# Taking an expert's quarters two at a time, and letting six experts add their rows in memory

## The chip, the cores and the metric

The kernel runs on one core of one Trainium2 chip. Its time is the device time of that core in microseconds (us), the median of several executions. TensorE is called PE here, VectorE DVE, ScalarE ACT, GpSimd POOL and SyncE SP, as in the profile.

## What is computed

The reference is one layer of an encoder for 1024 tokens of width 1024: a LayerNorm, an input projection that feeds three mixers (retention, S5, windowed attention), an output projection with a residual and a LayerNorm, and then the part that the change touches: 16 experts that each choose 128 tokens, with a hidden width of 2048, and a last LayerNorm over all tokens.

```python
aff = jax.nn.softmax(logits, axis=-1)
gates, idx = lax.top_k(jnp.swapaxes(aff, 1, 2), cap)
xs = x[bidx, idx]
hdn = jax.nn.silu(jnp.einsum('becd,edf->becf', xs, w_gate)) * jnp.einsum('becd,edf->becf', xs, w_up)
out = jnp.einsum('becf,efd->becd', hdn, w_down) * gates[..., None]
ffn = jnp.zeros_like(x).at[bidx, idx].add(out.astype(x.dtype))
h = layer_norm(DEEPNORM_ALPHA * h + ffn, ln2_g[l], ln2_b[l])
```

All in float32. A token may be chosen by several experts, or by none; their outputs add up.

## The kernel before

The first part (up to about 460 us) computes the LayerNorm, the projections, the mixers and the routing; the change leaves it alone. From there on 16 experts run one after the other, and nearly all the time is theirs.

**Pieces.** An expert's hidden width is cut into four *quarters* of 512 columns. A quarter is six *pieces* of weights of 1 MB each (128 partitions x 2048 float32): two of the gate matrix, two of the up matrix, two of the down matrix, 384 pieces in all. PE multiplies a piece with `mm3_piece` (line 2292): each product is made from a high and a low part of both operands, as high x high, low x high and high x low, so that a piece is 12 products of 128x512. So each weight piece has to be split first. SP loads it into one of five buffers `wraw` (`Experts.load`, line 2335), ACT copies it to a rounded type, the high half (`Experts.high`, line 2352), DVE subtracts that from the raw piece, the low half (`Experts.low`, line 2361). Six buffers `whl` hold split pieces, so the splitting runs up to six pieces ahead of PE; a new piece is loaded into a raw buffer as soon as the low half that read it is made. Six pieces at the start (`WHOLE`) go to PE unsplit, by `mm_whole` (line 2300).

**A quarter.** For quarter q, PE runs steps 0 to 3 (gate, gate, up, up of q) and then steps 4 and 5 (the two down pieces of quarter q-1), in `Experts.quarter`. Around the steps stand other pieces of work, put into lists by `plan(q)` as "before" or "after" step (q, s): the silu of the gate product on ACT after step 2 (line 2396), its product with the up product on DVE after step 3 (line 2402), and, ahead of the next quarter's first step, four transposes on PE that turn the 128x512 hidden values `hid` (`turned`, line 2275), split into high and low `hT` by ACT and DVE right after that step (lines 55 and 56). Splits of tokens use the same two lines. The down products of an expert's four quarters add up in two PSUM banks `y`.

**An expert's tokens.** In experts 0 to 7 the next expert's tokens are found by `expert_hot` (DVE, line 2238) and `expert_slots` (eight small products on PE, line 2247), and their rows `xs` are gathered from memory by an indirect DMA on POOL (`expert_rows`, line 2254). In the third quarter the rows are transposed in two halves, ahead of steps 1 and 2. Alongside, experts 1 to 7 find the tokens of the expert eight further on as well; experts 8 to 14 only gather the next expert's rows.

**An expert's output.** It must be added to the rows `acc_d` in memory, which start as the scaled residual. Experts 0 to 7 do this in the store (`expert_add`): ACT scales the two halves of `y` by the gates into `eo` (line 2486), and an indirect DMA on POOL adds them in memory (line 2487). From expert 8 on, the last LayerNorm begins as well, since rows that are not chosen again are final: one of eight tiles of 128 tokens is normed beside each expert (`final_norm`: loaded as `zz<-acc_d` by SP at line 2549, stored at line 2552), and each later expert rewrites the output rows of its own tokens. So experts 8 to 14 gather their rows (`final_rows`, line 2505), DVE adds the two halves of `y` to them (`last_sum`, line 2567), POOL stores the sum to `acc_d` plainly (line 2587), and the same rows are normed (`last_norm`: ACT for mean and variance, DVE for gain and shift) and scattered to the output by POOL (line 2572). Expert 15 ends the kernel with the same in parts.

**What sets the order.** Each engine runs its instructions in the order in which the program writes them. SP's queue holds, beside the weight loads, the loads and stores of `final_norm`; an instruction that waits there holds back everything behind it. POOL's queue holds all indirect DMAs and two small operations per norm. PSUM gives the experts two banks to `y`, three to gate and up (`gu`), and three to transposes and slot products (`tp`).

Of the kernel before, what the change touches and what calls it, by code (L numbers as in the profile page):

```python
# [20 lines left out]
P = 128  # L21
# [2281 lines left out]
class Experts:  # L2303
# [7 lines left out]
    WHOLE = 0, 4, 10  # L2311
    sort = None

    def __init__(self, K, I, O):
        self.K, self.I, self.O = K, I, O
        self.order = []
        for q in range(4 * E + 1):
            e, f = divmod(q, 4)
            if q < 4 * E:
                self.order += [I[n][e, f, half] for n in ("exp_w_gate", "exp_w_up") for half in range(2)]  # L2320
            if q:
                e, f = divmod(q - 1, 4)
                self.order += [I["exp_w_down"][e, f, half] for half in range(2)]
# [60 lines left out]

    def plan(self, q):

        K, nc, pool = self.K, self.K.nc, self.K.ex
        e, f = divmod(q, 4)
        at, box = self.at, {}

        def put(name, fn):
            return lambda: box.__setitem__(name, fn())
# [5 lines left out]
        def hidden():  # L2398
            self.hT[q] = [pool.tile([P, 4, P], F32R, name=f"hT{s}", bufs=2) for s in range(2)]
            split(K, *self.hT[q], box["tp"])  # L2400
        at(self.after, q, 2, silu)
        at(self.after, q, 3, lambda: nc.vector.tensor_tensor(self.h[q], self.h[q], self.pg[q][1], OP.mult))  # L2402
        turn = (q + 1, 0 if q else 1) if q < 4 * E - 1 else (q, 5)
        at(self.before, *turn, put("tp", lambda: turned(K, self.h[q], 0)))
        at(self.after, *turn, hidden)
        if f == 0 and e + 1 < E:
            late = ((q, 0), (q, 3), (q, 3), (q + 2, 1)) if e else ((q + 2, 3), (q + 2, 5), (q + 2, 5), (q + 3, 4))
            if e < E - LAST:
                at(self.after, *late[0], put("hot", lambda: expert_hot(K, e + 1)))
                at(self.before, *late[1], put("pt", lambda: expert_slots(K, e + 1, box["hot"])))  # L2410
                at(self.after, *late[2], put("xs", lambda: expert_gather(K, e + 1, box["pt"], True)))
            else:
                at(self.after, *late[2], put("xs", lambda: expert_rows(K, e + 1)))
            for half in range(2):
                q1, s1 = late[3][0], late[3][1] + half
                at(self.before, q1, s1, put(half, lambda half=half: turned(K, box["xs"], half * 4)))
                at(self.after, q1, s1, lambda half=half: self.tokens(e + 1, half, box[half]))
        if f == 2 and 0 < e < E - LAST:
            e2 = e + LAST
            at(self.after, q, 0, put("hot", lambda: expert_hot(K, e2)))  # L2420
            at(self.before, q, 3, put("pt", lambda: expert_slots(K, e2, box["hot"])))
            at(self.after, q, 3, lambda: expert_gather(K, e2, box["pt"]))
# [9 lines left out]
        if q >= 4 * (E - LAST) and f == 0:  # L2432
            at(self.after, q + 1, 3, lambda: final_rows(K, e))

    def quarter(self, q):
        K, nc = self.K, self.K.nc
        e, f = divmod(q, 4)
        steps = []
        if q < 4 * E:
            self.plan(q)  # L2440
            self.pg[q] = [K.pg.tile([P, 512], F32, name="gu", tag="gu") for _ in range(2)]
            if f == 0:
                self.py[e] = [K.py.tile([P, 512], F32, name="y", tag="y") for n in range(2)]
            for s in range(4):
                half = s % 2
                steps.append((s, [[self.pg[q][s // 2]]] * 4,
                              lambda half=half: [[self.xT[e][r][:, half * 4 + c, :] for c in range(4)] for r in range(2)],
                              half == 0, half == 1))
        if q:
            e1, f1 = divmod(q - 1, 4)  # L2450
            for half in range(2):
                steps.append((4 + half, [self.py[e1], self.py[e1]],
                              lambda half=half: [[self.hT[q - 1][r][:, half * 2 + c, :] for c in range(2)] for r in range(2)],
                              f1 == 0 and half == 0, f1 == 3 and half == 1))
        for s, outs, a, first, last in steps:
            for fn in self.before.pop((q, s), []):
                fn()
            if self.taken in self.whole:
                mm_whole(nc, outs, [self.xF[:, s % 2 * 4 + c, :] for c in range(4)], self.whl.pop(self.taken), first, last)
            else:  # L2460
                mm3_piece(nc, outs, a(), self.whl.pop(self.taken), first, last, self.taken == len(self.order) - 1)
            for fn in self.after.pop((q, s), []):
                fn()
            if self.sort and next(self.sort, self) is self:
# [311 lines left out]
```

## Time and profile before

| | |
|---|---|
| median of 3 executions | 1581.62 us (1580.8 to 1582.26) |
| the profiled execution's own time | 1577.74 us |
| its span, first to last instruction | 1576.0 us |
| DMA traffic | 507.33 MB, of it 461.88 MB read from HBM |
| low halves on DVE (line 2361) | 378 of 2288 ns, 858.0 us |
| high halves on ACT (line 2352) | 378 of 1919 ns, 724.6 us |
| landing of a weight piece after its issue | 7.7 to 8.5 us |

The busy times of the engines overlap; what counts is which engine ends last in each stretch. The profile gives for each engine its busy time, for each group of instructions the idle time just before them and what ended it, and for the DMA queues what they moved. One piece is 1 MB, so the weights alone are 384 of those megabytes, and they are loaded in the last 1100 us. "Clock" or PEclk is the share of full speed that PE was granted.

### The profile page before, as it was taken

How to read it: one execution, taken by the hardware profiler on the slowest of the kernel's cores; microseconds unless marked ns; L12 is line 12 of the kernel's file. 1: busy time of each engine (PE TensorE's matmuls, PEld its weight loads, DVE VectorE, ACT ScalarE, POOL GpSimd, SP SyncE). 2: the span in 40 equal slices, each digit the busy share in tenths (PEclk: the TensorE clock that was granted, in tenths of full speed). 3: DMA queues.
4: the chain of work that ended last, by engine and by line, in shares of the span. 5: the costliest groups of instructions: out<-in, count | busy, mean ns of one | idle time of the engine just before them, and what ended most of it. 6: DMA issues, size and time to landing. Idle time of an engine off the chain costs nothing.

```text
span 1576.0 us, 21110 instructions
## 1 busy us (share of the span) xinstructions
PE 1553.0 (99%) x7713; PEld 1276.4 (81%) x7713; DVE 1400.0 (89%) x1726; ACT 1124.0 (71%) x1294; POOL 189.9 (12%) x244
## 2 busy tenths in 40 slices
PE   8999999999999999999999999999999999999997
PEld 6888888788866888888888888888888888888786
DVE  7986865888878989999999998989999999999996
ACT  6744455877735777777777777777877778787873
POOL 4002111111110101010100101000201201020111
PEclk9999999999999999999999999999999999999999
DMA  6556478344268999999999999999999999999993
GB/s 235 180 171 145 113 228 252 98 135 125 86 234 348 389 383 400 397 389 383 382 380 369 378 402 371 403 409 415 406 422 410 418 412 417 414 415 392 398 418 155
DMA packets 101529, 507.33 MB, mean 322 GB/s; under 512 B 12976, under 2 KB 26032, under 8 KB 50736
## 3 DMA queue, kind: packets, MB, share of 16 engines
q1 hardware_dynamic: 85120, 475.03, 77.1%
q0 software_dynamic: 16304, 30.94, 6.9%
q8 instruction: 61, 1.00, 0.2%
q14 instruction: 44, 0.36, 0.1%
HBM read 461.88 MB, written 42.99 MB: 320 GB/s over the span
## 4 chain that ended last, share of the span: by engine, by line
PE 79%; DVE 7%; DMA 7%; issue 3%; ACT 3%; SPq 0%; POOL 0%; POOLq 0%; ACTq 0%; DVEq 0%
PE gu L2292 34%; PE y L2292 17%; PE mm L64 5%; PE mm L66 5%; PE mm L65 5%; DVE whl L2361 4%; DMA wraw<-in_exp_w_down 2%; PE tp L2275 2%; DMA wraw<-in_exp_w_up 2%; PE gu L2300 1%; ACT whl L2352 1%; PE po L1521 1%; DMA wraw<-in_exp_w_gate 1%; PE tp L1501 1%; PE at L1450 1%
## 5 line engine op out<-in xcount | busy, mean ns | idle before, releaser
L2361 DVE TENSOR_TENSOR whl<-wraw,whl 128x2048 fp32r<-128x2048 f32 x378 | 858.0, 2288 | 65.3 <-ACT whl L2352 63.0
L2352 ACT ACTIVATE whl<-wraw 128x2048 fp32r<-128x2048 f32 x378 | 724.6, 1919 | 243.4 <-PE gu L2292 86.8
L2292 PE MATMUL gu<-whl,xT 128*128 128x512 f32 x3000 | 712.3, 394 | 0.0
L2292 PEld LDWEIGHTS gu<-whl,xT 128*128 128x128 f32 x3000 | 555.4, 188 | 114.6 <-issue 1.0
L2292 PE MATMUL y<-whl,hT 128*128 128x512 f32 x1536 | 359.5, 389 | 0.0
L2292 PEld LDWEIGHTS y<-whl,hT 128*128 128x128 f32 x1536 | 288.0, 188 | 59.7
L2254 POOL DMA_INDIRECT xs<-h_d,index x15 | 29.9, 1994 | 454.0 <-PE y L2292 301.4
L64 PE MATMUL mm<-hT,whl 128*128 128x512 f32 x160 | 65.4, 409 | 0.0
L65 PE MATMUL mm<-hT,whl 128*128 128x512 f32 x160 | 62.6, 391 | 0.0
L66 PE MATMUL mm<-hT,whl 128*128 128x512 f32 x160 | 62.5, 391 | 0.0
L55 ACT ACTIVATE hT<-tp 128x512 fp32r<-128x512 f32 x76 | 43.8, 583 | 16.3 <-PE tp L2275 9.8
L64 PE MATMUL mm<-WO,yh 128*128 128x512 f32 x128 | 53.4, 417 | 0.0
L56 DVE TENSOR_TENSOR hT<-tp,hT 128x512 fp32r<-128x512 f32 x76 | 51.4, 683 | 1.9 <-ACT hT L55 1.5
L66 PE MATMUL mm<-WO,yl 128*128 128x512 f32 x128 | 50.7, 396 | 0.0
L65 PE MATMUL mm<-WO,yh 128*128 128x512 f32 x128 | 50.6, 395 | 0.0
L2402 DVE TENSOR_TENSOR hid<-hid,gu 128x512 f32<-128x512 f32 x64 | 43.6, 681 | 2.2 <-PE gu L2292 2.2
L2396 ACT ACTIVATE hid<-gu 128x512 f32<-128x512 f32 x64 | 37.2, 581 | 8.6 <-PE gu L2300 8.6
L64 PE MATMUL mm<-whl,hT 128*128 128x256 f32 (+1 forms) x120 | 42.8, 356 | 0.0
L2275 PEld LDWEIGHTS tp<-ident,hid 128*128 128x128 f32 x256 | 31.5, 140 | 11.4 <-DVE hid L2402 3.4
L66 PE MATMUL mm<-whl,hT 128*128 128x256 f32 (+1 forms) x120 | 40.3, 336 | 0.4 <-DVE hT L182 0.4
L2275 PE MATMUL tp<-ident,hid 128*128 128x128 f32 x256 | 38.5, 272 | 1.9 <-DVE hid L2402 1.8
L1461 DVE CUSTOM_DVE_ANT_0 S<-at,R,sink 128x384 f32<-128x384 f32 (+1 forms) x64 | 36.8, 578 | 3.9 <-PE at L1450 3.3
(445 smaller groups left out, 1795.5 us busy)
## 6 DMA issues: line engine op xcount, KB each, us to landing
wraw<-in_exp_w_up SPq DMA_DIRECT2D x128, 1024.0 KB, 8.5
wraw<-in_exp_w_down SPq DMA_DIRECT2D x128, 1024.0 KB, 8.1
wraw<-in_exp_w_gate SPq DMA_DIRECT2D x122, 1024.0 KB, 7.7
wraw<-in_w_in SPq DMA_DIRECT2D x8, 1024.0 KB, 5.8
whole<-in_exp_w_gate SPq DMA_DIRECT2D x6, 1024.0 KB, 8.3
q_d<-kst SPq DMA_DIRECT2D x32, 128.0 KB, 2.5
wraw<-in_w_out SPq DMA_DIRECT2D x4, 1024.0 KB, 7.1
qs<-q_d POOLq DMA_DIRECT2D x16, 256.0 KB, 3.6
```

Of the source, the lines that this page charges most:

```text
L55: nc.scalar.activation(hi, src, AF.Copy)
L56: eng.tensor_tensor(lo, src, hi.bitcast(F32), OP.subtract)
L64: nc.tensor.matmul(ps, a[0], b[0], start=start, stop=False)
L65: nc.tensor.matmul(ps, a[0], b[1], start=False, stop=False)
L66: nc.tensor.matmul(ps, a[1], b[0], start=False, stop=stop)
L1461: K.nc.vector.tensor_tensor_reduce(S[g][:, :W], K.at.pop((i, g))[:, :W], K.R[:, ro:ro + W], 2.0 ** -(h + 1), K.sink[:, h:h + 1], OP.add, O ...
L2275: K.nc.tensor.transpose(pt[:, c, :], src[:, (c0 + c) * P:(c0 + c + 1) * P], K.ident)
L2292: nc.tensor.matmul(ps, a[s][c], u[:, t, i * w:(i + 1) * w], start=first and id(ps) not in began, stop=last and left[id(ps)] == 0)
L2352: self.K.nc.scalar.activation(u[:, 0, :], self.raw[k1].rearrange("p a b -> p (a b)"), AF.Copy)
L2361: self.K.nc.vector.tensor_tensor(u[:, 1, :], raw, u[:, 0, :].bitcast(F32), OP.subtract)
L2396: nc.scalar.activation(self.h[q], self.pg[q][0], AF.Silu)
L2402: at(self.after, q, 3, lambda: nc.vector.tensor_tensor(self.h[q], self.h[q], self.pg[q][1], OP.mult))
```

## The change

**Order of the pieces.** `program()` writes the order of all pieces down. The first expert stays as it was, quarter by quarter (`SINGLE`). From its end on, two quarters are taken together: gate and up of q, gate and up of q+1, the down pieces of q-2, the down pieces of q-1, twelve steps that are still counted as (q, 0) to (q, 5) and (q+1, 0) to (q+1, 5). `place(q, s)` gives the step at which piece s of quarter q stands.

**Hidden values.** The silu comes right after the first up piece as before. The product of gate and up comes after the second up piece for the second quarter of a pair, and two steps later than that for the first. Both quarters' transposes stand ahead of the next pair's first step; the two splits follow after steps 1 and 3 of that pair. `run()` replaces `quarter()`; `ahead()` does what stood at the end of its loop, and after two steps of each pair (6 and 7 of twelve) holds DVE's low halves back by two pieces.

**Tokens.** Up to expert 8 the rows are transposed at the start and in the middle of the second pair of the expert before (`turns`); the slot products for the expert eight ahead stand in that middle too. The rows of experts 9 to 15 are gathered an expert earlier than before, and transposed at the starts of the two pairs of the expert before, beside the hidden values.

**Outputs.** Experts 8 to 13 now use `late_norm`: `expert_add` adds their two halves in the store, as experts 0 to 7 do, one step later POOL gathers the summed rows (line 2643); mean and variance follow in the next quarter's steps, gain, shift and the scatter (line 2630) in the one after that. Expert 14 keeps `last_norm`, a quarter later, with its rows gathered at line 2564. In `final_norm` the tile is loaded one step later, and shift and store come up to three steps later.

After the change the splits stand at lines 2351 (high) and 2360 (low), the weight load at 2334, `expert_add` at 2545 and 2546, the tile's load at 2608 and its store at 2611.

The diff, without most of the removed lines of `plan` and `quarter`, which stand in the listing above, and without the copies of old code:

```diff
@@ -2309,18 +2309,17 @@
     WHOLE = 0, 4, 10
+    SINGLE = 4
...
@@ -2382,14 +2381,40 @@
+    def program(self):
...
+        for q in range(self.SINGLE):
+            put(6 * q, q, 0, 4)
+            if q:
+                put(6 * q + 4, q - 1, 4, 2)
+        for q in range(self.SINGLE, 4 * E, 2):
+            put(6 * q, q, 0, 4)
+            put(6 * q + 4, q + 1, 0, 4)
+            if q > self.SINGLE:
+                put(6 * q + 8, q - 2, 4, 2)
+            put(6 * q + 10, q - 1, 4, 2)
+        for i in range(2):
+            put(24 * E + 2 * i, 4 * E - 2 + i, 4, 2)
+        return out
+
+    def place(self, q, s):
+
+        if q < self.SINGLE:
+            return q, s
+        o = 6 * (q - q % 2) + 4 * (q % 2) + s
+        return o // 6, o % 6
...
-        at(self.after, q, 2, silu)
-        at(self.after, q, 3, lambda: nc.vector.tensor_tensor(self.h[q], self.h[q], self.pg[q][1], OP.mult))
-        turn = (q + 1, 0 if q else 1) if q < 4 * E - 1 else (q, 5)
-        at(self.before, *turn, put("tp", lambda: turned(K, self.h[q], 0)))
-        at(self.after, *turn, hidden)
...
+        at(self.after, *self.place(q, 2), silu)
+        late = 2 * (q >= self.SINGLE and q % 2 == 0)
+        at(self.after, *self.place(q, 3 + late), lambda: nc.vector.tensor_tensor(self.h[q], self.h[q], self.pg[q][1], OP.mult))
+        if q < self.SINGLE:
+            t = (q + 1, 0 if q else 1)
+        elif q < 4 * E - 2:
+            t = (q - q % 2 + 2, 0)
+        else:
+            t = (4 * E - 1, 4)
+        at(self.before, *t, turn)
+        at(self.after, t[0], t[1] + (q == 4 * E - 1 if t[1] else q % 2 * 2 + 1 if q >= self.SINGLE else 0), hidden)
+
+    def others(self, q):
...
+        elif f == 0 and e < E - LAST:
+            slots(e + 1, (q, 0), (q, 3), True)
+            turns(e + 1, (q + 2, 0), (q + 3, 0))
+        elif f == 2 and E - LAST - 1 <= e < E - 2:
+            at(self.after, q, 3, put("xs", lambda: expert_rows(K, e + 2)))
+            turns(e + 2, (q + 2, 0), (q + 4, 0))
         if f == 2 and 0 < e < E - LAST:
...
+            slots(e + LAST, (q, 1), (q + 1, 0), False)
         if f == 0:
             if e < E - LAST:
-                at(self.after, q + 5, 0, lambda: expert_add(K, e, self.py[e]))
+                at(self.after, q + 6, 0, lambda: expert_add(K, e, self.py[e]))
+            elif e < E - 2:
+                late_norm(self, e)
             elif e < E - 1:
                 last_norm(self, e)
...
+    def run(self):
...
+                if step:
+                    self.ahead(2 * (q >= self.SINGLE and q % 2 == 1 and s < 2))
...
+    def ahead(self, hold=0):
...
+        lead = self.taken + self.lead(self.taken)
+        self.high(min(lead + 1, self.taken + self.RING))
+        self.low(lead - hold)
+        self.taken += 1
...
-    X.at(X.after, q, 0, load)
+    X.at(X.after, q, 1, load)
     X.at(X.after, q, 5, lambda: last_mean(K, b["z"], b["y"], b["s"]))
     X.at(X.after, q + 1, 0, lambda: last_var(K, b["z"], b["y"], b["s"]))
...
+    X.at(X.after, q + 1, 2, lambda: last_gain(K, b["z"], b["y"], b["s"]))
+    X.at(X.after, q + 1, 5, lambda: last_shift(K, b["y"], b["s"]))
+    X.at(X.after, q + 2, 0, store)
...
+def late_norm(X, e):
+
+    K, b, q = X.K, {}, 4 * e + 6
+
+    def rows():
+        b["z"], b["s"] = K.ex.tile([P, D], F32, name="eo", tag="xs", bufs=3), stats_tile(K)
+        K.nc.gpsimd.indirect_dma_start(out=b["z"], out_offset=None, in_=K.acc_dram,
+                                       in_offset=bass.IndirectOffsetOnAxis(ap=K.index[:, e:e + 1], axis=0))
...
+    X.at(X.after, q, 0, lambda: expert_add(K, e, X.py[e]))
+    X.at(X.after, q, 1, rows)
+    X.at(X.after, q + 1, 2, mean)
+    X.at(X.after, q + 1, 3, lambda: last_var(K, b["z"], b["y"], b["s"]))
+    X.at(X.after, q + 2, 0, lambda: last_gain(K, b["z"], b["y"], b["s"]))
+    X.at(X.after, q + 2, 3, lambda: last_shift(K, b["y"], b["s"]))
+    X.at(X.after, q + 2, 4, lambda: last_scatter(K, X.O, e, b["y"]))
```

PE's order in a late expert before, from the last down piece of one quarter through the transposes of hidden values (`tp<-ident,hid`) and of the next expert's rows (`tp<-ident,xs`); `gu` is gate or up, `y` down, `x4` means four such instructions in a row:

```order
L2292 MATMUL y<-whl,hT_11721 128x512 x4
L2275 MATMUL tp<-ident,hid 128x128 x4
L2292 MATMUL gu<-whl,xT_11368 128x512 x4
L2292 MATMUL gu<-whl,xT_11369 128x512 x4
L2292 MATMUL gu<-whl,xT_11368 128x512 x4
L2275 MATMUL tp<-ident,xs 128x128 x4
L2292 MATMUL gu<-whl,xT_11368 128x512 x4
L2292 MATMUL gu<-whl,xT_11369 128x512 x4
L2292 MATMUL gu<-whl,xT_11368 128x512 x4
L2275 MATMUL tp<-ident,xs 128x128 x4
```

And the same engine after the change, at the seam of two pairs in a late expert, from the last two down pieces on:

```order
L2292 MATMUL y<-whl,hT_11623 128x512 x4
L2292 MATMUL y<-whl,hT_11624 128x512 x4
L2292 MATMUL y<-whl,hT_11623 128x512 x8
L2292 MATMUL y<-whl,hT_11624 128x512 x4
L2292 MATMUL y<-whl,hT_11623 128x512 x4
L2275 MATMUL tp<-ident,xs 128x128 x4
L2275 MATMUL tp<-ident,hid 128x128 x8
L2292 MATMUL gu<-whl,xT_11155 128x512 x4
```

The transposes of two quarters' hidden values and of one half of the rows now stand together, and products are cut into by transposes once in twelve pieces.

SP's order around a tile's load before, where a name in brackets is a semaphore that the instruction waits for: DMAHW counts landings of SP's own loads, DVE the low halves that free a raw buffer, DMASW4 the landing of the plain store of the expert's sum, which POOL issues six steps earlier:

```order
L2335 DMA wraw<-in_exp_w_up 128x2048 [waits DMAHW0_49,DVE_49]
L2335 DMA wraw<-in_exp_w_up 128x2048 [waits DMAHW1_49,DVE_49]
L2335 DMA wraw<-in_exp_w_down 128x2048 [waits DMAHW2_49,DVE_49]
L2549 DMA zz<-acc_d 128x1024 [waits DMASW4_49]
L2335 DMA wraw<-in_exp_w_down 128x2048 [waits DMAHW3_49,DVE_49]
L2335 DMA wraw<-in_exp_w_gate 128x2048 [waits DMAHW4_49,DVE_49]
```

And after, where DMASW3 is the landing of the adding store that POOL issues one step earlier:

```order
L2334 DMA wraw<-in_exp_w_down 128x2048 [waits DMAHW6_49,DVE_49]
L2334 DMA wraw<-in_exp_w_down 128x2048 [waits DMAHW7_49,DVE_49]
L2334 DMA wraw<-in_exp_w_down 128x2048 [waits DMAHW0_49,DVE_49]
L2334 DMA wraw<-in_exp_w_down 128x2048 [waits DMAHW1_49,DVE_49]
L2608 DMA zz<-acc_d 128x1024 [waits DMASW3_49]
L2334 DMA wraw<-in_exp_w_gate 128x2048 [waits DMAHW2_49,DVE_49]
L2334 DMA wraw<-in_exp_w_gate 128x2048 [waits DMAHW3_49,DVE_49]
```

The tile's load now stands right behind an adding store of the same memory, ahead of the next expert's gate weights.

More of the change, by code (lines that the diff above doesn't have):

```diff
@@ L2315, in __init__ @@
         self.K, self.I, self.O = K, I, O
+        self.steps = self.program()
         self.order = []
-        for q in range(4 * E + 1):
+        for _, q, s in self.steps:
             e, f = divmod(q, 4)
[L2319 to L2323, printed above, removed]
+            self.order.append(I["exp_w_gate" if s < 2 else "exp_w_up"][e, f, s % 2] if s < 4 else
+                              I["exp_w_down"][e, f, s - 4])
         self.whole = [k + i for k in self.WHOLE for i in range(2)]
@@ L2431, in plan @@
                 final_norm(self, t, q + 4 * t + 2)
[L2432 to L2436, printed above, removed]
-        e, f = divmod(q, 4)
[L2438 to L2442, printed above, removed]
-                self.py[e] = [K.py.tile([P, 512], F32, name="y", tag="y") for n in range(2)]
[L2444 to L2464, printed above, removed]
-                self.sort = None
-                K.sorted()
-            lead = self.taken + self.lead(self.taken)
-            self.high(min(lead + 1, self.taken + self.RING))
-            self.low(lead)
-            self.taken += 1
-        self.pg.pop(q - 1, None), self.h.pop(q - 2, None), self.hT.pop(q - 2, None)
@@ new lines, in product @@
+    def product(self, q, s):
+        K, nc, half = self.K, self.K.nc, s % 2
+        e, f = divmod(q, 4)
+        if s < 4:
+            if s == 0:
+                self.pg[q] = [K.pg.tile([P, 512], F32, name="gu", tag="gu") for _ in range(2)]
+            outs, a = [[self.pg[q][s // 2]]] * 4, [[x[:, half * 4 + c, :] for c in range(4)] for x in self.xT.get(e, [])]
+            first, last = half == 0, half == 1
+        else:
+            if f == 0 and s == 4:
+                self.py[e] = [K.py.tile([P, 512], F32, name="y", tag="y") for n in range(2)]
+            outs, a = [self.py[e]] * 2, [[x[:, half * 2 + c, :] for c in range(2)] for x in self.hT[q]]
+            first, last = f == 0 and half == 0, f == 3 and half == 1
+        if self.taken in self.whole:
+            mm_whole(nc, outs, [self.xF[:, half * 4 + c, :] for c in range(4)], self.whl.pop(self.taken), first, last)
+        else:
+            mm3_piece(nc, outs, a, self.whl.pop(self.taken), first, last, self.taken == len(self.order) - 1)
@@ L2708, in build @@
     K.sorted = sorted_out
-    for q in range(4 * E + 1):
-        X.quarter(q)
+    X.run()
     last_rows(X, E - 1)
```

74 lines of the change are left out of this document (49 added, 25 removed).

## The prediction

> **What bounds the kernel now.** I read the page's engine table and slices first, then busy time by stretches one expert long, then the chain of work inside one expert, and last the rows of the engines around one expert's store.
>
> ```profile
> PE 1553.0 (99%) x7713; PEld 1276.4 (81%) x7713; DVE 1400.0 (89%) x1726; ACT 1124.0 (71%) x1294; POOL 189.9 (12%) x244
> PE   8999999999999999999999999999999999999997
> PEclk9999999999999999999999999999999999999999
> DMA  6556478344268999999999999999999999999993
> ```
>
> TensorE (PE) is busy in every slice and its granted clock never falls; from a third of the span on, the DMA engines are busy all the time too. The stretches below run from one quarter's first product to the same product of the next expert, so each holds one expert's work: one early expert, then four late ones in a row.
>
> ```profile
> core 0: us, PE busy (x) PEld busy (x) DVE busy (x) ACT busy (x) POOL busy (x), PEclk, DMA share, GB/s
> 720.56:789.48 68.92, 68.92 (x330) 56.65 (x329) 63.26 (x47) 51.95 (x37) 4.96 (x2) 1.00 0.99 378
> 1217.82:1286.07 68.25, 68.25 (x314) 56.41 (x313) 65.35 (x41) 54.77 (x43) 10.72 (x8) 1.00 1.01 416
> 1286.07:1355.07 69.00, 69.00 (x317) 57.01 (x316) 66.15 (x41) 55.55 (x43) 10.50 (x8) 1.00 1.01 416
> 1355.07:1424.07 69.00, 68.46 (x313) 56.34 (x312) 64.83 (x41) 53.65 (x43) 9.99 (x8) 1.00 1.01 410
> 1424.07:1493.08 69.01, 67.71 (x310) 55.74 (x309) 64.84 (x41) 54.99 (x43) 8.61 (x7) 1.00 1.01 403
> ```
>
> Until 1286 us PE has no idle time: the expert costs what PE's instructions cost, 68.25 us. The next three take 207.01 us together, 2.26 more than three times 68.25, with 1.84 us of it as plain idle time. PE's waits from 1400 us on are one row:
>
> ```profile
> PE tp L2275 <- DVE hid L2402: 1.8, 2, 1.3
> ```
>
> PE stood before the transposes of a quarter's hidden values, whose product of gate and up VectorE (DVE) had not yet made. DVE is at 65 of 68 us there, and the quarter gives it two pieces (5.4 us) from the up product to the transposes.
>
> So two limits lie close together: PE, and the feeding of PE (weight load, ACT's high half, DVE's low half). This chain is one late expert on PE, from the quarter in which the next expert's rows are transposed:
>
> ```profile
> 1182.76 0.44 PE tp L2275 x4
> 1183.20 2.78 PE gu L2292 x12
> 1185.98 0.44 PE tp L2275 x4
> 1186.41 2.77 PE gu L2292 x12
> 1189.19 0.44 PE tp L2275 x4
> 1189.63 5.50 PE gu L2292 x24
> 1195.13 5.44 PE y L2292 x24
> 1200.57 0.44 PE tp L2275 x4
> 1201.01 10.93 PE gu L2292 x48
> 1211.94 5.44 PE y L2292 x24
> 41.31 0.87 PE tp L204 x8
> ```
>
> A piece is 12 products and takes 2.72 us undisturbed (5.44 / 2). Behind a group of transposes the first piece takes 2.77 or 2.78: each break between transposes and products costs about 0.06. The last row, from early in the program, shows that eight transposes in a row cost 0.87, twice four, and no more.
>
> **The change, term by term. First, breaks on PE.** Products and transposes stay the same in number. Before, an expert has six breaks (four quarters, two halves of the next expert's rows); now a pair of quarters begins with all its transposes. A late pair is 12 transposes, 0.44 + 0.87, then 96 gate-up products, 10.93 + 10.88 (48 behind a break, 48 without its 0.05), and 48 down products, 2 x 5.44: 34.00 us. Two pairs are 68.0 against 68.25. Over experts 1 to 15 the change removes 30 breaks before hidden values (one a pair) and 28 before rows (in the early experts one of the halves stands beside the slot products, which break there anyway): 58 x 0.06 = 3.5 us, all on PE, which is the bound. **-3.5.**
>
> **Second, slack for the hidden values.** Now the product of gate and up is ordered two pieces after the first quarter's up product, at the second one's own, and the transposes come with the next pair: at least four pieces (10.9 us) instead of two. The splits of the transposed values have some seven pieces until the down products read them. What made PE wait 2.26 us (1.84 idle, the rest drawn out) has no place left, as long as the feeding itself isn't late. **-2.3.**
>
> **Third, the sums of experts 8 to 13.** DVE's two sums go, ACT's two scalings come:
>
> ```profile
> L2567 DVE SCALAR_TENSOR_TENSOR eo<-y,gates,eo 128x512 f32<-128x512 f32 x16 | 11.3, 744 | 5.5 <-PE y L2292 5.5
> L2486 ACT ACTIVATE eo<-y,gates 128x512 f32<-128x512 f32 x16 | 10.0, 673 | 0.0
> L2238 DVE TENSOR_TENSOR hot<-slot,slots 128x512 bf16<-128x512 f32 x30 | 19.3, 683 | 0.0
> L56 DVE TENSOR_TENSOR hT<-tp,hT 128x512 fp32r<-128x512 f32 x76 | 51.4, 683 | 1.9 <-ACT hT L55 1.5
> ```
>
> An expert's DVE load falls by 2 x 0.744 = 1.5 us, ACT's rises by 1.35 of the 13 it has free: nothing on the path by itself. But the store must now add in memory, and the tile load `zz<-acc_d` (line 2608) has moved from 6 pieces behind the store to one. It is issued by SP, on the one queue that also issues every weight load, and must wait for the store to land. The nearest rows are those around expert 7's store, which adds in memory today (the first two from the chain, the next six from the timeline, the last two the landings of the adding store and of a weight load from their lines' views):
>
> ```profile
> 1029.44 0.44 PE tp L2275 x4
> 1029.87 10.94 PE gu L2292 x48
> 1029.47 1.92 ACT L2352 ACTIVATE whl<-wraw 128x2048 fp32r<-128x2048 f32 x1 [0.80 <-PE y L2292]
> 1031.30 1.25 ACT L2486 ACTIVATE eo<-y,gates 128x512 f32<-128x512 f32 x2
> 1031.42 2.29 DVE L2361 TENSOR_TENSOR whl<-wraw,whl 128x2048 fp32r<-128x2048 f32 x1 [0.42 <-ACT whl L2352]
> 1032.82 2.35 POOL L2487 DMA_INDIRECT acc_d<-eo,index  x1 [63.39 <-ACT eo L2486]
> 1033.74 3.77 SPq L2335 DMA_DIRECT2D wraw<-in_exp_w_down  x2
> 1039.68 3.04 SPq L2335 DMA_DIRECT2D wraw<-in_exp_w_gate  x2
> 1045.20 0.33 SPq L2335 DMA_DIRECT2D wraw<-in_exp_w_up  x1
> 1045.20 0.99 POOL L2505 DMA_INDIRECT eo<-acc_d,index  x1 [10.03 <-DMA acc_d<-eo,index]
> DMA to landing us min/median/max: 11.0/11.7/12.9
> DMA to landing us min/median/max: 4.8/8.1/17.2
> ```
>
> POOL waits for the landing until 1045.2. In the new order SP would stand there as well: the last weight load ahead of it goes out at 1037.2 (33.74 + 3.77, less 0.33 for one issue), the ones of 1039.7 and 1042.4 would go at 1045.6. That is a hole of 8.0 us in the issues. The load of 1037.2 keeps the DMA engines fed for about 9 (8.1 typical, more beside the store); the load behind the hole brings its data some 2.3 after its issue (the fastest landing of 4.8 less 2.5 for 1 MB at full rate). So the engines idle for 8.0 + 2.3 - 9 = 1.3 us an expert, between 0.9 and 2.5.
>
> Can the DMA engines afford that? Two stretches at the same full share:
>
> ```profile
> 1472.00:1488.00 16.00, 16.00 (x74) 13.21 (x73) 14.23 (x9) 12.62 (x11) 1.73 (x2) 1.00 1.02 427
> 1030.00:1044.00 14.00, 14.00 (x63) 11.58 (x62) 12.40 (x8) 11.08 (x9) 2.35 (x1) 1.00 1.02 386
> ```
>
> 427 GB/s is full rate; with an adding store in it the stretch moves 386, so adding costs 14 x 41 / 427 = 1.3 us of all engines. A late expert moves 416 x 68.25 = 28.4 MB, 66.5 us at 427, now 67.8 with the adding. PE wants 68.0. The feeding loses 1.3 (hole) less 0.2, about 1.1 us an expert, and falls behind by that much at each of the eight tile loads: some 9 by the end, or less, since the more it lags the longer its queue and the shorter the idle time.
>
> What covers that lag is the row of split pieces. In the rows above PE ends a piece at 1029.44 and ACT starts a high half in its buffer at 1029.47; PE reads that buffer again as its sixth piece from there, at 1029.87 + 10.94 + 2.72 = 1043.5, and DVE has its low half at 1033.71: 9.8 us ahead. Before, the hidden values spent that cover first (the wait above came at a small lag); now nothing is due sooner. Nine of lag in 9.8 of cover: I take a wait of 0.8 us in all, with bounds of 0 (idle for 0.9: 0.7 x 8 = 5.6, covered) and 9 (idle for 2.5: 2.3 x 8 = 18.4, less 9.8).
>
> [...]
>
> **Sum.** -3.5 - 2.3 + 0.8 = -5.0 us. The profiled execution took 1577.74 (its span 1576.0 and 1.74 around it), which gives 1572.7. The runs' median is 1581.62, 3.9 above the profiled one; I take that difference as unchanged, so 1576.6 for the median. A measurement of this kernel can tell about 0.2% from no change, 3.2 us.
>
> **Rivals.** *The hole starves PE.* The place is SP before `zz<-acc_d`; the price is the lag beyond the cover. Every microsecond of loss an expert above 9.8 / 8 = 1.2 puts 8 us on the end; from (9.8 + 5.8) / 8 = 1.95 the kernel is slower than before. At 2.7 (the slowest store's 12.9, which makes the idle time 2.5, and engines that fall short of PE's pace by 0.2 instead of beating it by that) it is 21.6 - 9.8 - 5.8 = +6.0: 1587.6. For it: full DMA share today, and a queue that can't pass the waiting load. [...] Against it: the lag feeds the queue. Chance 0.18.
>
> *The gain is handed back in small waits*: in experts 1 to 7 the slot products of the expert eight ahead, in the middle of the second pair, take the bank that held the second hidden values, and so wait for their split on DVE. In line from the first piece's end stand three low halves (2.29 each), the hot rows (2 x 0.683) and two splits; the third low half starts no sooner than two pieces on, so the split ends about 11.5 us on, and the bank is wanted at 13.6. Two of slack cover it, and a lag above that doesn't; in expert 1, where weights come late, it may cost 1 to 3 us once, and 0.7 each in seven experts would take 5. Time then 1579 to 1582, no change. The same end has a partly starved PE (3 to 6 us). Chance 0.22.
>
> **Numbers.** Forecast 0.60, its own range 1574.3 (both gains, no wait, some of the unprofiled runs' longer time gone too) to 1578.4. No change 0.22, slower 0.18. The range of 8 in 10 goes from 1574.3 to 1585.5, which leaves out the worst of the starved case. Faster by over 0.2%: 0.60; within: 0.22; slower: 0.18.
>
> **What would show it.** Right: a late expert of about 68.0 on PE, an early one of 68.65; no wait of `tp` for `hid`; SP's issues with a hole of about 8 us at each `zz<-acc_d`, and ACT waiting longer for weights behind it. Wrong: PE waiting for `whl` from DVE in the last experts (the hole starves), or the slot products waiting in experts 1 to 7.

## The result and the profile after

The changed kernel takes 1600.78 us (1593.6 to 1605.77, 6 runs), the kernel before 1582.08 (1580.8 to 1584.48, 6 runs): 18.7 us slower, a ratio of 1.0127 with a 95% interval of 1.0108 to 1.0146 (the quotient of the two medians, 1.0118, lies inside). Forecast were 1576.6. The profiled execution took 1603.88, with a span of 1602.2, and stands 26.1 above the profiled one before, somewhat more than the medians do.

The page's engine table and slices of the changed kernel:

```profile
PE 1561.3 (97%) x7713; PEld 1283.6 (80%) x7713; DVE 1393.4 (87%) x1714; ACT 1131.2 (71%) x1306; POOL 203.1 (13%) x244
PE   8999999999999999999999999999999998999995
DMA  5556478343178999999999999999999999999993
```

PE still looks full, but for the same 7713 instructions its busy time is 8.3 us longer: some products are drawn out or run at a lower granted clock (0.94 in the last stretch). The stretches say where. The first holds an early expert, the next five the experts 10 to 14, each from the first product of its second quarter to the same product of the next expert (us, busy time of each engine, clock, DMA share, GB/s):

```profile
743.06:811.69 68.63, 68.63 (x329) 56.93 (x328) 63.18 (x47) 52.05 (x36) 4.95 (x2) 1.00 0.99 382
1155.27:1223.28 68.01, 68.01 (x313) 56.58 (x312) 60.24 (x35) 51.95 (x42) 13.02 (x8) 1.00 1.00 395
1223.28:1292.42 69.14, 68.20 (x314) 56.56 (x312) 62.21 (x38) 53.13 (x43) 12.04 (x8) 1.00 1.00 395
1292.42:1366.98 74.56, 70.42 (x313) 57.52 (x312) 66.43 (x40) 57.90 (x46) 13.09 (x8) 0.98 0.99 393
1366.98:1436.40 69.42, 68.20 (x314) 56.57 (x313) 62.78 (x38) 53.94 (x44) 12.53 (x8) 1.00 1.00 394
1436.40:1507.76 71.36, 69.66 (x309) 55.58 (x308) 62.53 (x38) 54.93 (x44) 13.10 (x8) 1.00 1.00 393
```

The early expert takes 68.63 and the first of the late ones 68.01: PE's own instructions became as much cheaper as forecast. But the DMA engines move 393 to 395 GB/s at a full share, where it was 403 to 416 before, and after 1223 us four experts take 284.5 us instead of four times 68. The end, the last 305 products and transposes, before (first fence) and after:

```profile
1498.39:1565.76 67.37, 67.37 (x305) 55.39 (x303) 57.94 (x38) 44.35 (x35) 9.21 (x8) 1.00 0.77 319
```

```profile
1507.76:1591.97 84.21, 73.73 (x305) 57.75 (x303) 69.53 (x45) 51.36 (x41) 13.85 (x9) 0.94 0.76 299
```

The end alone loses 16.8 us. Three queues now wait where they did not before, except for two waits of POOL's, 11.5 us together (from the waits of SP and ACT after 1000 us and of POOL):

```profile
SPq L2608 <- DMA acc_d<-eo,index: 56.9, 8, 8.4
ACT zz L2582 <- DMA zz<-acc_d: 16.2, 8, 4.2
POOL eo L2643 <- DMA acc_d<-eo,index: 47.1, 5, 10.5
```

SP stands 7.1 us (56.9 / 8) before a tile's load; then ACT stands before the tile's mean, and its high halves of weights behind it. One such place, in expert 12 (timeline rows of POOL, SP, ACT and PE):

```profile
1327.12 2.38 POOL L2546 DMA_INDIRECT acc_d<-eo,index  x1 [16.53 <-ACT eo L2545]
1328.05 3.28 SPq L2334 DMA_DIRECT2D wraw<-in_exp_w_down  x2
1339.75 0.33 SPq L2608 DMA_DIRECT2D zz<-acc_d  x1
1340.17 0.87 SPq L2334 DMA_DIRECT2D wraw<-in_exp_w_gate  x2
1340.01 1.92 ACT L2351 ACTIVATE whl<-wraw 128x2048 fp32r<-128x2048 f32 x1 [3.87 <-DMA wraw<-in_exp_w_down]
1343.32 1.06 ACT L2582 ACTIVATE zz<-zz 128x1024 f32<-128x1024 f32 x1 [1.40 <-DMA zz<-acc_d]
1346.81 2.11 PE L2292 MATMUL y<-whl,hT 128*128 128x512 f32 x8 [1.19 <-ACT whl L2351]
1353.95 0.66 PE L2275 MATMUL tp<-ident,xs 128*128 128x128 f32 x4 [2.74 <-DMA xs<-h_d,index]
```

No weight load goes out between 1331.3 and 1340.2. ACT waits 3.87 us for a weight piece and 1.40 for the tile. PE then stands before a split piece, and again before the rows `xs`, whose gather went out at 1341.30, held up on POOL behind the gather that waits 10.49 us for the same store.

At the end it is worse. SP's rows around the last tile's load, and PE's two longest stands (timeline), then the landing of a last piece (from the chain):

```profile
1546.03 3.85 SPq L2334 DMA_DIRECT2D wraw<-in_exp_w_down  x2
1557.95 0.33 SPq L2608 DMA_DIRECT2D zz<-acc_d  x1
1558.37 3.01 SPq L2334 DMA_DIRECT2D wraw<-in_exp_w_down  x4
1567.23 1.11 PE L2275 MATMUL tp<-ident,hid 128*128 128x128 f32 x4 [3.64 <-DVE hid L2431]
1577.44 2.08 PE L2292 MATMUL y<-whl,hT 128*128 128x512 f32 x4 [2.76 <-ACT hT L55]
```

```profile
1561.04 13.84 DMA wraw<-in_exp_w_down
```

The last four weight loads stand behind that tile, which waits 8 us for expert 14's store. ACT and DVE take their work in the order written: the silu of the last hidden values (1565.29) comes behind the tile's mean, before which ACT waits 4.20 us, and the splits of hidden values (L55, 1576.81) come behind three high halves that wait 1.36, 1.63 and 0.51 us for their loads. PE stands behind both, for 3.64 and 2.76 us.

### The profile page after: what moved, and what is told of

The parts are those of the page before. It is cut to its first block, busy times and chain, and to the rows that moved or that the text cites. A ratio compares the mean times of both kernels' runs of the same rounds, so it can differ in the third digit from the quotient of the medians.

```text
span 1602.2 us, 21127 instructions
## 1 busy us (share of the span) xinstructions
PE 1561.3 (97%) x7713; PEld 1283.6 (80%) x7713; DVE 1393.4 (87%) x1714; ACT 1131.2 (71%) x1306; POOL 203.1 (13%) x244
## 4 chain that ended last, share of the span: by engine, by line
PE 63%; DMA 17%; DVE 9%; issue 5%; ACT 5%; POOL 0%; SPq 0%; POOLq 0%; ACTq 0%; DVEq 0%
PE gu L2292 24%; PE y L2292 12%; DVE whl L2360 6%; DMA wraw<-in_exp_w_gate 5%; PE mm L64 5%; PE mm L66 5%; PE mm L65 5%; DMA acc_d<-eo,index 4%; DMA wraw<-in_exp_w_up 3%; DMA wraw<-in_exp_w_down 2%; PE tp L2275 2%; ACT whl L2351 2%; PE gu L2300 1%; PE po L1521 1%; PE tp L1501 1%
## 5 line engine op out<-in xcount | busy, mean ns | idle before, releaser
L2292 PE MATMUL gu<-whl,xT 128*128 128x512 f32 x3000 | 698.5, 392 | 2.9 <-ACT hid L2421 1.5
L2546 POOL DMA_INDIRECT acc_d<-eo,index x14 | 32.6, 2328 | 332.1 <-ACT eo L2545 332.1
L55 ACT ACTIVATE hT<-tp 128x512 fp32r<-128x512 f32 x76 | 43.7, 583 | 11.6 <-PE tp L204 6.7
L2630 POOL DMA_INDIRECT out<-yl,index x8 | 31.3, 3912 | 117.4 <-DVE hT L56 93.5
```

Of the source, the lines that this page charges most:

```text
L55: nc.scalar.activation(hi, src, AF.Copy)
L2292: nc.tensor.matmul(ps, a[s][c], u[:, t, i * w:(i + 1) * w], start=first and id(ps) not in began, stop=last and left[id(ps)] == 0)
L2546: nc.gpsimd.indirect_dma_start(out=K.acc_dram, out_offset=bass.IndirectOffsetOnAxis(ap=K.index[:, e:e + 1], axis=0), in_=o, in_offset=None ...
```

## The experiments

The theory after this profile: the *hole* on SP (the time in which it issues no load) starves PE. The rival: the *adding* stores take so much of the DMA engines that the weights come late wherever the tile's load stands. A third, the *pairs* themselves, came in when both were found to be true and not enough.

The ratio in each row is against the kernel before, in runs on the same chip; different rows can come from different chips, so rows are compared by their ratios. A ratio can differ from the quotient of the medians by some 0.1%. Store to load and load to mean are counted in steps of one piece (2.7 us). "Lows held" is the holding back of low halves in `ahead()`. add_plain and the three thin kernels are measurements only: add_plain leaves the sum out, the thin ones leave most of each tile unwritten.

| kernel | order | sums of experts 8 to 13 | store to tile's load | load to mean | lows held | median us | ratio (95%) |
|---|---|---|---|---|---|---|---|
| before | quarters | DVE | 6 | 5 | no | 1582.08 | 1 |
| after | pairs | adding | 1 | 4 | yes | 1600.78 | 1.0127 (1.0108 to 1.0146) |
| late_tile | pairs | adding | 5 | 4 | yes | 1612.31 | 1.0197 (1.0174 to 1.0221) |
| plain_sum | pairs | DVE | 1 | 4 | yes | 1604.43 | 1.0138 (1.0119 to 1.0158) |
| before_hole | quarters | DVE | 1 | 10 | no | 1597.24 | 1.0103 (1.0082 to 1.0124) |
| before_add | quarters | adding | 6 | 5 | no | 1603.23 | 1.0133 (1.0108 to 1.0158) |
| before_mean | quarters | DVE | 6 | 3 | no | 1598.68 | 1.0112 (1.0087 to 1.0137) |
| pairs_alone | pairs | DVE | 5 | 4 | no | 1592.55 | 1.0059 (1.0037 to 1.0080) |
| hold_alone | pairs | DVE | 5 | 4 | yes | 1597.72 | 1.0096 (1.0075 to 1.0117) |
| no_hold | pairs | adding | 1 | 4 | no | 1597.27 | 1.0091 (1.0062 to 1.0120) |
| add_alone | pairs | adding | 5 | 4 | no | 1609.43 | 1.0168 (1.0139 to 1.0197) |
| pairs_spaced | pairs | DVE | 6 | 5 | no | 1587.10 | 1.0049 (1.0029 to 1.0068) |
| hold_spaced | pairs | DVE | 6 | 5 | yes | 1585.26 | 1.0025 (1.0006 to 1.0044) |
| add_spaced | pairs | adding | 6 | 5 | no | 1600.72 | 1.0130 (1.0107 to 1.0154) |
| add_plain | pairs | plain store, later norm | 6 | 5 | no | 1590.32 | 1.0059 (1.0043 to 1.0075) |
| pairs_tail | pairs | DVE | 6 | 5 | no | 1587.25 | 1.0031 (1.0017 to 1.0046) |
| pairs_tail_rows | pairs | DVE | 6 | 5 | no | 1586.60 | 1.0032 (1.0015 to 1.0049) |
| pairs_thin | as pairs_spaced, less stored | | | | | 1583.08 | 1.0011 (1.0000 to 1.0023) |
| after_thin | as after, less stored | | | | | 1594.89 | 1.0085 (1.0062 to 1.0108) |
| before_thin | as before, less stored | | | | | 1577.53 | 0.9977 (0.9965 to 0.9989) |

**The four first: each suspect by itself.**

late_tile, on the changed kernel:

```diff
-    X.at(X.after, q, 1, load)
-    X.at(X.after, q, 5, lambda: last_mean(K, b["z"], b["y"], b["s"]))
+    X.at(X.after, q, 5, load)
+    X.at(X.after, q + 1, 3, lambda: last_mean(K, b["z"], b["y"], b["s"]))
...
```

> The changed kernel, with one thing moved: each tile's load stands four steps later on SP's queue, five steps (13.6 us) behind the expert's store, so that the store has landed (11 to 12 us) when SP comes to it; mean, variance, gain, shift and the tile's store follow later. The adding stores and the pairs stay. Theory of the hole (SP stands 7 us before each tile's load, weight loads behind it come late, and PE starves): SP's wait before zz goes to nearly 0, the last experts take 68.0 to 68.3 us each instead of 69 to 74, the end loses its waits, and the time is 1576 to 1580. Theory of the adding (the adding stores take so much of the DMA engines that the weights come late, wherever the tile's load stands): still above 1590.

plain_sum, on the changed kernel (and `final_rows` for experts 8 to 14 again):

```diff
-            elif e < E - 2:
-                late_norm(self, e)
```

> The changed kernel without its third part: experts 8 to 13 gather their rows, sum on DVE and store plainly, as before; the pairs stay, and the tile's load still stands one step behind the store. Theory of the hole: SP stands nearly as long (a plain store lands in about 10 us instead of 11.5), the feeding loses a microsecond or two an expert, and the time stays above 1588. Theory of the adding: without adding stores the DMA engines have their time back, and it is 1576 to 1582.

before_hole, on the kernel before:

```diff
-    X.at(X.after, q, 0, load)
+    X.at(X.after, q - 1, 1, load)
```

> The kernel before, with one line moved: each tile's load stands one step behind the expert's store instead of six. No pairs, no adding store after expert 7. Theory of the hole: SP stands 6 to 8 us before each tile's load, and the kernel goes from 1582 to 1588 to 1600. Theory of the adding, or of the pairs as the cause: no change, 1580 to 1584.

before_add, on the kernel before (with `late_norm` copied in, a quarter earlier):

```diff
+            elif e < E - 2:
+                late_norm(self, e)
             elif e < E - 1:
                 last_norm(self, e)
```

> The kernel before, with the changed kernel's third part alone: experts 8 to 13 add in the store, gather the sums and norm them later; quarters one at a time, and the tile's load six steps behind the store. No hole. Theory of the hole: 1580 to 1586, the adding alone costs 1.4 us of the DMA engines an expert and PE's cover of 9 us takes most of that. Theory of the adding: above 1590.

Neither theory holds alone. Without the hole the changed kernel is slower still (1612.31), without adding stores no faster (1604.43; SP stands 8.2 us there before a tile's load, 65.5 / 8, and in the kernel before plain stores land 8.1 to 8.8 us behind their issue). Yet on the order of before the hole alone costs 16 us (1597.24 against 1581.22 on that chip) and the adding alone 22. In before_hole SP's wait is there (first fence); in before_add there is none, and five late experts move 388 to 399 GB/s, as in the changed kernel (second fence):

```profile
SPq L2549 <- DMA acc_d<-eo,index: 45.9, 8, 6.2
```

```profile
1090.27:1164.48 74.21, 70.26 (x314) 57.48 (x312) 65.89 (x41) 55.34 (x44) 10.79 (x7) 0.98 0.99 388
1164.48:1233.96 69.48, 68.43 (x314) 56.35 (x312) 63.26 (x37) 55.58 (x44) 11.66 (x7) 1.00 1.00 399
1233.96:1306.95 72.99, 70.20 (x313) 57.43 (x312) 66.25 (x41) 55.57 (x44) 17.72 (x9) 0.98 1.00 397
1306.95:1376.68 69.73, 68.46 (x314) 56.34 (x312) 63.32 (x37) 55.78 (x44) 13.82 (x8) 1.00 0.99 396
1376.68:1451.20 74.52, 70.15 (x313) 57.48 (x312) 66.26 (x41) 55.68 (x44) 11.77 (x8) 0.98 0.99 389
```

So each one is enough to make the feeding the bound, and their prices don't add up. That also hid a third: ACT's stand before the tile's mean, which is 14.8 us in late_tile too.

**The next four: pairs without the three.** pairs_alone is late_tile with plain_sum's edit and this one; hold_alone is the same without it, no_hold is the changed kernel with it alone, add_alone is late_tile with it:

```diff
-                    self.ahead(2 * (q >= self.SINGLE and q % 2 == 1 and s < 2))
+                    self.ahead()
```

> The changed kernel with three things taken back: sums and plain store for experts 8 to 13 as before (no adding after expert 7), the tile's load five steps behind the store (no hole), and no holding back of low halves. What is left is the order in pairs. If each of the three lengthens the way from a load's issue to the low half that frees its buffer, and five such buffers then pace the loads: the loads come every 2.85 us again, the late experts take 68.0, and the time is 1574 to 1579. If the pairs themselves are the trouble (their bursts of splits and products on DVE and ACT): above 1590.

> The same with the low halves held back again in steps 6 and 7 of each pair. If holding back costs (two loads of each pair go out some 5 us late, and DVE stands before the second quarter's product meanwhile): 1588 to 1600, with low halves that start over 2 us behind their high halves. If it is free: as pairs_alone within 3 us.

> The changed kernel with only the holding back undone; adding stores and the hole stay. If the hole and the adding are the larger part: 1592 to 1600, hardly better than the changed kernel. If holding back is the larger part: 1580 to 1588.

> Pairs with the adding stores of experts 8 to 13, but without the hole and without holding back. If the adding alone takes the DMA engines beyond what they have (its 1.4 us an expert and more in the landings around it): 1588 to 1600, as on the order of before (1603). If the hole or the holding back explain the slow late_tile: 1576 to 1583.

The medians with the low halves held back are 3 to 5 us longer, but the intervals overlap, so that price isn't shown; it would be only a part of the loss. Adding costs 17 us again (1609.43 against 1592.55). The pairs without both are 0.59% slower than before, although PE runs without a wait there from 1080 to 1320 us. But in pairs_alone and its kin my edit had left the mean four steps behind the load, as the changed kernel has it, and without a hole ahead of it the tile's load landed 10.6 us after its issue, not 3.7 (medians). ACT stood there for twice the changed kernel's 16.2 us:

```profile
ACT zz L2580 <- DMA zz<-acc_d: 32.6, 8, 5.0
```

The kernel before, with five steps, never waits there.

**The third four: the mean where it was, and that stand by itself.** pairs_spaced is pairs_alone with the tile's chain as far from the store as before:

```diff
-    X.at(X.after, q, 5, load)
-    X.at(X.after, q + 1, 3, lambda: last_mean(K, b["z"], b["y"], b["s"]))
+    X.at(X.after, q + 1, 0, load)
+    X.at(X.after, q + 1, 5, lambda: last_mean(K, b["z"], b["y"], b["s"]))
...
```

hold_spaced and add_spaced are hold_alone and add_alone with the same edit.

> As pairs_alone (pairs, plain sums, no holding back), with the tile's chain placed as the kernel before has it against the store: load six steps behind the store, mean five steps behind the load. In pairs_alone the mean stood four steps behind, ACT waited 32.6 us in eight times for tiles, and every high half behind it waited too; the lag grew by 1.2 us an expert. If that stand on ACT is what the pairs alone lost: no wait of ACT for zz, lag under 3, late experts of 68.0, 1574 to 1579. If the order in pairs itself feeds more slowly: the lag grows again and the time stays above 1587.

> pairs_spaced with low halves held back in steps 6 and 7 of each pair. Holding back costs what hold_alone showed against pairs_alone (about 5 us): 1579 to 1585. If its price depended on the stand of ACT only: as pairs_spaced within 2 us. If the held loads starve the DMA engines: above 1588.

> pairs_spaced with the adding stores and the late norm of experts 8 to 13 in place of plain sums. On the order of before they cost 21 us without any hole. If adding in memory takes that from the DMA engines wherever it stands: 1592 to 1602. If it was the interplay with the tight hidden values of the order before: 1576 to 1584.

before_mean, on the kernel before:

```diff
-    X.at(X.after, q, 5, lambda: last_mean(K, b["z"], b["y"], b["s"]))
+    X.at(X.after, q, 3, lambda: last_mean(K, b["z"], b["y"], b["s"]))
```

> The kernel before, with the tile's mean two steps earlier, three steps behind its load instead of five. ACT comes to it before the tile (9.4 us to landing) is there and stands some 3 to 5 us in each of eight experts, with high halves behind it. If a stand on ACT is passed on to PE: 1586 to 1600. If ACT's free time (13 us an expert) takes it: 1580 to 1584.

One number moved by two costs the kernel before 1.12% (before_mean). ACT's waits there:

```profile
ACT zz L2523 <- DMA zz<-acc_d: 41.5, 8, 6.1
```

5.2 us in each of eight experts, on an engine that is free for 13: the free time doesn't help, since the high halves stand behind the mean in ACT's queue. In pairs_spaced that wait is gone and holding back costs nothing (hold_spaced is if anything faster). Adding still costs 13.6 us. Between pairs_spaced and pairs_alone the intervals overlap, so what the stand cost there isn't settled.

**The last six: what adding costs, and where pairs still lose.** add_plain is add_spaced with a plain store in `late_norm` (`op` is a new argument of `expert_add`):

```diff
-                                 in_=o, in_offset=None, compute_op=OP.add)
+                                 in_=o, in_offset=None, **({} if op else {"compute_op": OP.add}))
...
-    X.at(X.after, q, 0, lambda: expert_add(K, e, X.py[e]))
+    X.at(X.after, q, 0, lambda: expert_add(K, e, X.py[e], 1))
```

> add_spaced with one thing changed: experts 8 to 13 store their scaled rows plainly over the old ones instead of adding them in memory (this leaves the sum out; the bytes, the waits and the later norm of these rows stay). If the adding itself takes the DMA engines' time (13.6 us in six experts, add_spaced against pairs_spaced): back to 1585 to 1589. If the price lies in the later norm's places, its gather behind the store and POOL's waits: still 1597 to 1602.

pairs_tail, on pairs_spaced (and its split right behind step (64, 0)):

```diff
-            t = (4 * E - 1, 4)
+            t = (4 * E - 1, 4) if q % 2 == 0 else (4 * E, 0)
```

> pairs_spaced with the last quarter's transposes two pieces later than the ones of the quarter before it, ahead of the first of the last two down pieces' pairs. In pairs_spaced PE stood 4.8 us longer than its instructions before the last pair's transposes, since DVE had low halves of late weights ahead of the last product of gate and up, and the next piece took 2.3 us longer. If that stand is most of what pairs_spaced loses: 1579 to 1583. If the lag of the feeding only turns up at the next place: 1585 to 1588.

pairs_tail_rows, on pairs_tail:

```diff
-            at(self.after, q, 3, put("xs", lambda: expert_rows(K, e + 2)))
+            at(self.after, q, 0, put("xs", lambda: expert_rows(K, e + 2)))
```

> pairs_tail with the rows of experts 9 to 15 gathered three steps earlier, on POOL's queue ahead of the gather that waits for the expert's store. PE stood up to 1.3 us twice for these rows, and more in the changed kernel (5.9 us in four times). If these stands count beside the tail: 1 to 3 us less than pairs_tail, 1576 to 1581. If not: as pairs_tail.

The thin kernels, on pairs_spaced, on the changed kernel and on the one before:

```diff
-        ins = K.nc.sync.dma_start(X.O["out"][t * P:(t + 1) * P, :], b["y"])
+        ins = K.nc.sync.dma_start(X.O["out"][t * P:(t + 1) * P, 0:P], b["y"][:, 0:P])
```

> pairs_spaced with each tile's store cut to its first 128 of 1024 columns (this leaves seven eighths of eight tiles of the output unwritten): 0.46 of about 28.4 MB an expert less to move, every instruction and wait in its place. In pairs_spaced the lag grew by 0.7 us an expert from 1100 us on. If the DMA engines' time is what the feeding lacks, 0.46 MB give back 1.1 us an expert (at 416 GB/s): no growing lag, no wait of PE in the last experts, 1575 to 1580. If DVE's and ACT's order sets the pace of the feeding: as pairs_spaced, 1585 to 1589.

> The changed kernel with the same cut of the tiles' stores. It loses some 3 us an expert in the last six. If the DMA engines' time is short, 1.1 us an expert comes back: 1590 to 1595. If the holes and stands alone set its time: as the changed kernel, 1598 to 1603.

> The kernel before with the same cut. Its lag is near 0 until 1400 us and PE waits 2.3 us in all after that. If the DMA engines' time is short there only at the end: 1578 to 1581, the waits gone. If PE alone bounds it: no change, 1581 to 1583.

Of the 13.6 us, 10.4 are the adding itself (1600.72 to 1590.32): 1.7 us for each of six stores. The rest, 3.2, isn't clear of noise (1.0059 against 1.0049, the intervals overlap). One store's 12 us, from 5 us behind its issue, in add_spaced and then in add_plain:

```profile
1191.52:1203.52 12.00, 12.00 (x54) 9.94 (x53) 10.23 (x8) 8.97 (x8) 3.43 (x2) 1.00 1.03 379
1191.57:1203.57 12.00, 12.00 (x55) 9.93 (x54) 11.39 (x8) 10.10 (x8) 5.03 (x2) 1.00 1.02 425
```

The six such stretches move 374 to 380 GB/s with the adding and 423 to 427 without it, at the same full share: 1.4 us of all DMA engines' time for each store (12 x 48.5 / 425).

pairs_tail and pairs_tail_rows fell as theories: PE's waits only moved. In all three thin kernels less traffic gives time back, 3.6 to 5.9 us (before_thin came out faster than both of its expectations), so the bytes cost time in each of them, in the kernel before too. But pairs_thin stays 5.5 us behind before_thin, and both move the same bytes, so the pairs lose something else as well. ACT and DVE in pairs_thin, in the second half of a pair:

```profile
1159.81 1.92 ACT L2351 ACTIVATE whl<-wraw 128x2048 fp32r<-128x2048 f32 x1 [0.52 <-DMA wraw<-in_exp_w_down]
1162.26 1.92 ACT L2351 ACTIVATE whl<-wraw 128x2048 fp32r<-128x2048 f32 x1
1162.08 0.68 DVE L56 TENSOR_TENSOR hT<-tp,hT 128x512 fp32r<-128x512 f32 x1
1162.68 4.49 DVE L2360 TENSOR_TENSOR whl<-wraw,whl 128x2048 fp32r<-128x2048 f32 x2
1167.08 0.68 DVE L56 TENSOR_TENSOR xT<-tp,xT 128x512 fp32r<-128x512 f32 x1
1167.68 0.68 DVE L2431 TENSOR_TENSOR hid<-hid,gu 128x512 f32<-128x512 f32 x1
1168.28 4.48 DVE L2360 TENSOR_TENSOR whl<-wraw,whl 128x2048 fp32r<-128x2048 f32 x2
1171.32 1.92 ACT L2351 ACTIVATE whl<-wraw 128x2048 fp32r<-128x2048 f32 x1 [1.98 <-DMA wraw<-in_exp_w_up]
```

The high half that starts at 1162.26 is done at 1164.18; its low half starts at 1168.28, 4.1 us later, because DVE's splits and products of a pair stand together there and DVE runs without a pause. The raw buffer comes free that much later, its next load goes out that much later, and at 1171.32 ACT in turn waits 1.98 us for weights. Over all pieces from 1090 to 1490 us a low half starts 1.86 us after the end of its high half on average, in before_thin 0.93. This chain is read from the trace; no run moved those instructions apart, so it isn't shown by an experiment.

No version of pairs beat the kernel before with the same output; the nearest, hold_spaced, is 0.25% slower.

## Why the prediction was wrong, by its own steps

- **Breaks on PE** (-3.5): right. An early expert 68.63 (forecast 68.65), a late one 68.01 (68.0). One stand of 1.4 us at the first transposes of expert 8 was not foreseen; the profile names nothing that ended it.
- **Slack for the hidden values** (-2.3): its condition, "as long as the feeding itself isn't late", failed, so the gain can't be seen. The feeding was late, and PE again waits for them, 5.3 us in two times, both in the last pair, where the new order leaves only two pieces from product to transposes.
- **The hole on SP**: its place and size were right (8.0 forecast, 7.1 measured, 8.4 at most), and its price in DMA time nearly so: in before_hole the 12 us from 5 us behind a store move 334 to 369 GB/s (mean 355), in the kernel before 402 to 428 (mean 421), which is 1.9 us a hole where 1.3 were forecast, with 2.5 as the upper bound. Eight of them are 15 us, nearly all of the 16 that the hole costs there: neither reserve nor cover took it up.
- **The adding store** (1.3 us of all engines): its DMA time was right (1.4, from add_spaced and add_plain); in time it cost 1.7 (add_plain), so all of it and more reached the end.
- **The failed step** is the reserve of 0.2 us an expert in "The feeding loses 1.3 (hole) less 0.2, about 1.1 us an expert". It took 427 GB/s, from one stretch of 16 us, as a rate that a whole expert can have; its rows show no whole expert above 416. The 12 us from 5 us behind a store's issue, and the rest up to the next store, in the changed kernel and then in the kernel before:

```profile
1187.86:1199.86 12.00, 12.00 (x54) 9.94 (x54) 8.95 (x5) 7.06 (x8) 1.97 (x2) 1.00 0.96 336
1199.86:1261.25 61.39, 61.39 (x285) 51.09 (x284) 55.67 (x34) 48.68 (x39) 9.72 (x6) 1.00 1.00 399
1176.82:1188.82 12.00, 12.00 (x59) 9.88 (x58) 11.57 (x7) 9.99 (x9) 5.78 (x4) 1.00 1.02 425
1188.82:1245.25 56.43, 56.43 (x258) 46.66 (x257) 53.89 (x34) 45.00 (x34) 5.02 (x5) 1.00 1.00 414
```

In the changed kernel six such stretches of 12 us move 304 to 352 GB/s (mean 333). Against 427 that is 2.6 us each, the prediction's 1.3 and 1.3: hole and adding together were sized right. But the rest moves 399 to 412 (mean 407), and 397 to 417 in the kernel before, not 427. By these rows a late expert's 28.4 MB take an estimated 72 us (12 at 333, 60 at 407), 4 over PE's 68.0, where the prediction lost 1.1. That before_thin gains 3.6 us and has none of PE's waits in the experts says the same: the kernel before had no reserve in its last experts. What holds the rate at 407, the DMA engines or raw buffers that ACT and DVE free late, isn't settled.
- **Three terms were missing.** The rows `xs` were held up on POOL, where PE stood 4.9 us in three times. The mean one step nearer to its load makes ACT stand (16.2 us in all; two steps nearer cost the kernel before 17 us). And pairs_thin is 5.5 us slower than before_thin, though the pairs need 0.25 us less of PE in a late expert; that DVE's bunched work delays the loads there is a reading of the trace, not shown by a run.
- **The cover** of 9.8 us was counted once for eight experts. PE first stands before a split piece at 1346 us, behind the fifth hole; from there on little cover was left, and at the end the last hidden values come due with the weights: the end lost 16.8 us where the sum had nothing.
- **The rivals**: "the hole starves PE" named the sign and the place, and its price of 2.7 an expert was too low by what the terms above add. The slot products of the early experts cost nothing, as the 68.63 of the first stretch shows.

What stays open: why the changed kernel is faster with its hole (no_hold, 1.0091) than without (add_alone, 1.0168) when stores add; and how the loss splits between hole, adding, ACT's stand and the pairs where all are present.

## What to carry to other kernels

In a late expert of the kernel before (68.25 us) PE is busy all the time, DVE for 65.35 us, and the DMA engines' share is 1.01. With engines as close together as that, the 0.24 us an expert gained on PE (68.25 to 68.01) were worth less than the spacing that keeps the loads issuing: the hole alone cost 16 us (before_hole), and the mean two steps nearer to its load 17 (before_mean), although ACT is free for 13 us an expert. So count each wait on a queue that works in order (SP, ACT, DVE here) with all the weight traffic behind it, even when that engine has free time. A full DMA share said nothing of reserve here (it was 0.99 at 378 GB/s in an early expert and 1.02 at 427 in a stretch of 16 us): take the rate that a whole period of the kernel moves, not the best of a short stretch, or cut some traffic and see. And cover that held a lag in the middle of this kernel was gone at its end, where the changed kernel lost 16.8 us.

## What the runs showed of the hardware

Some stands of PE cost more than their length here. After the stands of expert 12 (1.19, 0.21 and 2.74 us) and at the end, the granted clock in short stretches is (the first row is an earlier stand):

```profile
1005.00:1010.00 5.00, 3.61 (x23) 2.98 (x22) 4.98 (x3) 2.24 (x2) 0.00 (x0) 1.00 0.99 395
1350.00:1354.00 4.00, 1.26 (x11) 0.93 (x9) 3.71 (x3) 2.76 (x3) 0.00 (x0) 1.00 1.03 424
1354.00:1358.00 4.00, 4.00 (x14) 3.22 (x15) 2.79 (x2) 3.44 (x6) 0.00 (x0) 0.63 1.01 426
1576.00:1582.00 6.00, 4.19 (x9) 2.90 (x10) 5.50 (x5) 1.88 (x3) 0.00 (x0) 0.58 0.02 10
```

0.63 over 4 us is an estimated 1.5 us lost (4 x 0.37), on top of the 4.1 us of standing before it. In steps of 1 us the granted clock is 1.00 from 1354 on, then 0.53, 0.50, 0.50 and 0.77, and 1.00 again from 1359; at the end it is 0.96 from 1576 on and 0.50 in each of the five steps from 1577 to 1582. Around the single stand of 1.4 us (first row) it stayed at 1.00. Which length of stand goes with such a fall isn't shown: no single stand before the 0.63 was longer than 2.74 us, and no run varies the length.
